# Opening's step 0 loaded as x with slab 0's weights, then the other three slabs', each by SyncE and ScalarE in halves of the rows; slab 0's products first

## The chip, the cores and the metric

The kernel runs on one NeuronCore of a Trainium2 chip. The metric is the device time of one execution in microseconds. All data are float32.

## The reference, cut to what matters

One inference step of a decoder with two layers, for 256 prompt tokens (T) and 8 sample tokens (B), so N = 264 columns of x, each of 1024 features. Layer 0 is a gated short convolution, layer 1 block-sparse attention with a paged cache. The change touches only the start of layer 0 and one store of keys:

```
b_gate, c_gate, h, z = split(x @ w_in, 4, axis=-1)      # w_in: 1024 x 4096
u = c_gate * h
conv = sum(w_conv[j] * up[:, j:j + T] for j in range(3)) # up: earlier rows, then u
y = (b_gate * conv * silu(z)) @ w_out
x = layernorm(alpha * x + y)
...                                                      # layer 1; its new keys k are an output
```

## The kernel before

**Products.** Features lie on the 128 partitions, tokens along the free dimension. Every weight matrix is cut into slabs of 128 output features, 80 in all, numbered n = 0 to 79; a slab holds 8 blocks of 128 x 128, one for each 128 input features (k = 0 to 7). A float32 product is made of three: each operand is split into a high part (a cast to a shorter form, `hi` for weights, `m0h` in the profile for x) and a low part (what is left, `lo` and `m0l`), and high x high, high weight x low x and low weight x high x are added up in PSUM. The casts to the high part are mostly ScalarE's (`act.copy`), the low parts are subtractions on VectorE (`dve.tensor_sub`).

**The opening.** Slabs 0 to 3 and x come together. The tensor `first` has 8 steps k; step k holds 128 rows of 264 columns of x (feature block k) and 4 x 128 columns of the weights of slabs 0 to 3 for that block. Step k needs 12 products: 4 slabs by 3 parts, added to four accumulators. Step 0 and step 1 are each loaded in two pieces by columns, one issued by SyncE (L191, L194) and one by ScalarE (L192, L194); steps 2 to 7 are one DMA each on SyncE's queue (L196). Then come the constants (L197), the page table (L198) and the loads of slabs 4 to 7 (`load`, L112). `first_split(k)` writes the casts of a step in order: x high (L218), weight highs (L222, `high`), x low (L210, `x_low`), weight lows (L225, `low`). The loop over k at L471 then writes TensorE's products: high weights by x high and x low at L475, low weights by x high at L478. Each engine runs its own instructions in the order written.

**Ahead of it** `keep_warm(WARM)` gives TensorE eight products of 512 bf16 columns on constants (L80), with no use of their result.

**After it** `begin(n)` and `mm` go slab by slab (n = 4 to 79) over a table of slots: `at(n, phase, f)` puts a step f into slot n, and `begin(n)` runs the phases of that slot in a fixed order ("dma" first). TensorE's products of slab n are at L139 to L141, the casts of a later slab at L127 (high, ScalarE) and L132 (low, VectorE). With S = 40, `k_store(h, n)` stores the rotated keys of n heads from head h on, on SyncE's queue (L640); heads 2 and 3 go together at slot S + 18, the others singly, head 6 at S + 21 and head 7 at S + 22.

Of the kernel before, what the change touches and what calls it, by code (L numbers as in the profile page):

```python
# [21 lines left out]
N = T + B  # L22
# [2 lines left out]
NPAGE = 20  # L25
ALPHA = math.sqrt(2.0)
EPS = 1e-5
WARM = 8
NKV = 10
EARLY = (40, 41, 42)  # L30
LATE = (78, 79)
# [18 lines left out]
def build(tc, a):  # L50
    nc = tc.nc
    pe, act, dve, pool, sp = nc.tensor, nc.scalar, nc.vector, nc.gpsimd, nc.sync

    with ExitStack() as top:
# [10 lines left out]
        def acc_tile():  # L65
            return acc_full()[:, 0:N + 2]
# [10 lines left out]
        def keep_warm(n):  # L77
            wt = big_tile("warmp")
            for _ in range(n):
                pe.matmul(wt[:, 0:512], one[:, 0:128], one, start=True, stop=True)  # L80

        keep_warm(WARM)

# [20 lines left out]
        raws, his, los = {}, {}, {}  # L104
# [41 lines left out]
        def at(n, phase, f, *args):  # L146
            hooks.setdefault((n, phase), []).append(lambda: f(*args))
# [31 lines left out]
        def begin(n, end=True):  # L179
            for ph in ("dma", "pe", "s0", "hi", "lo", "s1a", "s1b", "s1", "s1c"):  # L180
                run(n, ph)
            if end:
                split_late(n)
# [4 lines left out]


        fst = [ex.tile([128, N + 512], F32, name=f"first{k}") for k in range(8)]  # L190
        sp.dma_start(fst[0][:, 0:N + 128], a["first"][0, :, 0:N + 128])  # L191
        act.dma_start(fst[0][:, N + 128:], a["first"][0, :, N + 128:])  # L192
        for eng, c in ((sp, np.s_[:, 0:N + 256]), (act, np.s_[:, N + 256:])):
            eng.dma_start(fst[1][c], a["first"][1][c])  # L194
        for k in range(2, 8):
            sp.dma_start(fst[k], a["first"][k])  # L196
        sp.dma_start(cst[:, 0:C_ID], a["cst"][:, 0:C_ID])  # L197
        sp.dma_start(pt, a["pt"])  # L198
# [10 lines left out]
        def x_low(k):  # L209
            dve.tensor_sub(pair[0][1][:, k, 0:N], fst[k][:, 0:N], pair[0][0].bitcast(F32)[:, k, 0:N])  # L210

        def first_split(k):
            if k % 2 == 0:
                for d, c in ((his, "hi"), (los, "lo")):
                    d[k // 2] = wp.tile([128, 8, 128], F32R, tag=c, bufs=6, name=f"{c}{k // 2}")
            h, l = his[k // 2], los[k // 2]
            r = 4 * (k % 2)
            act.copy(pair[0][0][:, k, 0:N], fst[k][:, 0:N])  # L218
            raw = fst[k][:, N:].rearrange("p (s m) -> p s m", m=128)

            def high(eng, s0, s1):
                eng(h[:, r + s0:r + s1], raw[:, s0:s1])  # L222

            def low(s0, s1):
                dve.tensor_sub(l[:, r + s0:r + s1], raw[:, s0:s1], h.bitcast(F32)[:, r + s0:r + s1])  # L225

            if k == 0:
                high(dve.tensor_copy, 0, 1)
                high(dve.tensor_copy, 1, 2)
                high(act.copy, 2, 4)  # L230
            elif k == 1:
                high(act.copy, 0, 2)
                high(act.copy, 2, 4)
            elif k == 2:
                high(dve.tensor_copy, 0, 2)
                high(act.copy, 2, 4)
            else:
                high(act.copy, 0, 4)
            x_low(k)
            for s0, s1 in ((0, 2), (2, 4)) if k < 2 else ((0, 4),):  # L240
                low(s0, s1)

        for k in range(8):
            first_split(k)
# [224 lines left out]
        accs = [acc_tile()[:, 0:N], acc_tile()[:, 0:N], two[:, 0:N], two[:, 512:512 + N]]  # L469
        cs_prep()  # L470
        for k in range(8):  # L471
            mh, ml = pair[0][0][:, k, 0:N], pair[0][1][:, k, 0:N]
            for s, c in [(s, c) for c in range(2) for s in range(4)] if k in (0, 2) else [(s, c) for s in range(4) for c in range(2)]:
                wh = his[k // 2][:, (k % 2) * 4 + s, :]
                pe.matmul(accs[s], wh, (mh, ml)[c], start=k == 0 and c == 0, stop=False)  # L475
            for s in range(4):
                wl = los[k // 2][:, (k % 2) * 4 + s, :]
                pe.matmul(accs[s], wl, mh, start=False, stop=k == 7)  # L478
        begin(3)
        ORDER = (2, 1, 3, 0)  # L480
        for s in range(4):
# [56 lines left out]
        with tc.tile_pool(name="l1", bufs=1) as p1, ExitStack() as late_pool:  # L538
# [324 lines left out]
            S = 40  # L863
# [6 lines left out]
                at(S + (11, 11, 12, 12, 15, 15, 16, 16)[h], "s1", rows_back, 0, h)  # L870
                at(S + (13, 13, 14, 14, 18, 19, 20, 21)[h], "s1", rows_back, 1, h)
            for h in range(8):
                if h not in (2, 3):
                    at(S + (15 if h < 4 else 19) + h % 4, "dma", k_store, h)
                at(S + 18 + h, "dma", v_store, h)

            at(S + 18, "dma", k_store, 2, 2)
            at(S + 3, "s1", zero_fill)
            for h0, n, ph in ((0, 6, "s0"), (4, 8, "s1")):
                at(S + n, ph, s_rope, qs, h0, h0 + 4)  # L880
# [194 lines left out]
            for i in range(2, 32):  # L1075
# [13 lines left out]
                h = i % 8  # L1089
# [51 lines left out]
            for k in range(8):  # L1141
                for c in range(2):
                    for j in range(4):
                        pe.matmul(ps[32 * j:32 * j + 32], gs[:, c, k, :],  # L1144
                                  wide(raws, k)[:, 256 * j + 128 * c:256 * j + 128 * c + 128],
                                  start=k == 0 and c == 0, stop=False)
# [93 lines left out]
```

## Time and profile before

| | us |
|---|---|
| median of 3 runs | 275.22 (275.09 to 276.06) |
| the profiled execution's own time | 275.37 |
| its span | 273.6 |
| TensorE busy in the span | 268.7 |
| VectorE, ScalarE, GpSimd busy | 203.0, 170.9, 65.9 |
| mean DMA rate over the span | 243 GB/s |

Times in profile rows count from the start of the span. A row of the timeline has start, duration, engine, line of the code, operation, output <- inputs and count, and in brackets how long the engine had been idle and what ended that. SPq is SyncE's queue of DMA issues; a row of it is the issue, not the transfer. PE is TensorE, PEld its weight loads, ACT ScalarE, DVE VectorE, POOL GpSimd. Matmuls are pipelined: a row's duration is longer than the pitch between two of them.

### The profile page before, as it was taken

Reading aid. Unit: us, or ns where it says so; the run is one execution under the profiler, and the core shown is the slowest. Engines: PE = TensorE matmul, PEld = TensorE weight load, DVE = VectorE, ACT = ScalarE, POOL = GpSimd, SP = SyncE. Lnnn points to the kernel's source line nnn. Section 1 sums busy time; section 2 is a strip of 40 time slices with the busy share of each in tenths; the row PEclk is TensorE's granted clock in tenths of the full one; section 3 lists DMA queues with packets and bytes.
Section 4 is the critical chain, followed back from the end, with each engine's and each line's share of the span. In section 5 each row is a group of like instructions: output and inputs, shape, how many; then the busy total and the mean of one; then the engine's idle time right before and its main releaser. Section 6 shows DMA issues by size and latency. Waiting matters only on the chain.

```text
span 273.6 us, 6278 instructions
## 1 busy us (share of the span) xinstructions
PE 268.7 (98%) x2307; PEld 251.9 (92%) x2307; DVE 203.0 (74%) x414; ACT 170.9 (62%) x349; POOL 65.9 (24%) x129
## 2 busy tenths in 40 slices
PE   8999999999999999999999999999999999999994
PEld 5999999999999999999997997999959987998883
DVE  3978966655875857979999858699847583994745
ACT  4886554453655628549587765988846954599302
POOL 1121432020110101961323365621100020000122
PEclk9999999999999999999999999999999999999999
DMA  7976789999775875132223999997989955781012
GB/s 246 409 274 225 268 291 320 399 396 379 244 257 196 278 234 188 57 149 77 80 77 101 364 404 386 357 338 235 351 320 305 407 195 172 237 276 61 1 77 89
DMA packets 24336, 66.48 MB, mean 243 GB/s; under 512 B 3058, under 2 KB 6898, under 8 KB 24178
## 3 DMA queue, kind: packets, MB, share of 16 engines
q1 hardware_dynamic: 23874, 65.69, 67.6%
q10 hardware_dynamic: 432, 0.39, 0.5%
q8 instruction: 18, 0.29, 0.4%
q14 instruction: 12, 0.10, 0.1%
HBM read 61.67 MB, written 3.35 MB: 238 GB/s over the span
## 4 chain that ended last, share of the span: by engine, by line
PE 96%; DMA 2%; ACT 0%; SPq 0%; DVE 0%; issue 0%
PE acc L139 24%; PE acc L141 24%; PE acc L140 24%; PE c L1023 4%; PE sd L758 3%; PE dps L809 3%; PE acc L475 2%; PE acc L1023 2%; PE c1b L1023 2%; DMA first<-first 2%; PE so L1144 1%; PE acc L478 1%; PE s L692 1%; PE o L730 1%; PE pt L720 1%; PE s L690 1%
## 5 line engine op out<-in xcount | busy, mean ns | idle before, releaser
L127 ACT CAST hi<-raw 128x1024 fp32r<-128x1024 f32 x76 | 79.2, 1050 | 34.0 <-DMA raw<-w 18.9
L132 DVE TENSOR_TENSOR lo<-raw,hi 128x1024 fp32r<-128x1024 f32 x76 | 92.7, 1227 | 6.7 <-ACT hi L127 6.2
L139 PE MATMUL acc<-m0h,hi 128*128 128x264 f32 (+1 forms) x280 | 79.4, 283 | 0.0
L141 PE MATMUL acc<-m0l,hi 128*128 128x264 f32 (+1 forms) x280 | 79.3, 283 | 0.0
L140 PE MATMUL acc<-m0h,lo 128*128 128x264 f32 (+1 forms) x280 | 78.9, 282 | 0.0
L139 PE MATMUL acc<-m1h,hi 128*128 128x264 f32 x264 | 76.4, 289 | 0.0
L141 PE MATMUL acc<-m1l,hi 128*128 128x264 f32 x264 | 74.6, 282 | 0.0
L140 PE MATMUL acc<-m1h,lo 128*128 128x264 f32 x264 | 74.5, 282 | 0.0
L140 PEld LDWEIGHTS acc<-m0h,lo 128*128 128x128 f32 x280 | 52.7, 188 | 0.0
L139 PEld LDWEIGHTS acc<-m0h,hi 128*128 128x128 f32 x280 | 52.6, 188 | 0.1
L141 PEld LDWEIGHTS acc<-m0l,hi 128*128 128x128 f32 x280 | 52.5, 188 | 0.0
L139 PEld LDWEIGHTS acc<-m1h,hi 128*128 128x128 f32 x264 | 49.6, 188 | 1.7 <-issue 0.8
L140 PEld LDWEIGHTS acc<-m1h,lo 128*128 128x128 f32 x264 | 49.8, 189 | 0.0
L141 PEld LDWEIGHTS acc<-m1l,hi 128*128 128x128 f32 x264 | 49.6, 188 | 0.0
L431 POOL COPY uo<-up 128x10 f32<-128x10 f32 x8 | 8.0, 1003 | 64.2 <-DVE up L430 58.4
L648 POOL COPY vs<-vh 128x8 f32<-128x8 f32 x8 | 3.3, 408 | 32.5 <-ACT vh L647 32.5
L701 DVE CUSTOM_DVE_ANT_0 P<-s,cst 128x128 f32<-128x128 f32 (+1 forms) x16 | 5.1, 354 | 5.8 <-PE s L692 5.8
L439 DVE SCALAR_TENSOR_TENSOR t<-up,cst,t 128x256 f32<-128x256 f32 x8 | 3.9, 482 | 7.1 <-ACT t L438 7.1
L838 POOL COPY zs<-z 128x8 f32<-128x8 f32 x8 | 3.0, 377 | 24.4 <-ACT z L837 24.4
L837 ACT ACTIVATE z<-acc 128x264 f32<-128x264 f32 x8 | 3.1, 385 | 9.1 <-PE acc L141 9.1
L965 ACT ACTIVATE zq<-raw 128x1024 f32<-128x1024 f32 x8 | 8.5, 1058 | 0.1
L591 POOL COPY qs<-q 128x8 f32<-128x8 f32 x7 | 4.0, 577 | 17.7 <-ACT q L590 13.0
(230 smaller groups left out, 443.6 us busy)
## 6 DMA issues: line engine op xcount, KB each, us to landing
raw<-w SPq DMA_DIRECT2D x76, 512.0 KB, 4.6
kv<-kc SPq DMA_DIRECT2D x32, 256.0 KB, 6.0
kv<-vc SPq DMA_DIRECT2D x16, 512.0 KB, 6.7
first<-first SPq DMA_DIRECT2D x6, 388.0 KB, 6.7
v_o<-vh SPq DMA_DIRECT2D x8, 132.0 KB, 5.5
xf<-kall SPq DMA_DIRECT2D x16, 64.0 KB, 2.6
kall<-gb SPq DMA_DIRECT2D x1, 1024.0 KB, 6.0
k_o<-kall SPq DMA_DIRECT2D x6, 132.0 KB, 4.5
```

The lines of the kernel that those rows point to most:

```text
L127: act.copy(his[n][sl], raws[n][sl])
L132: dve.tensor_sub(los[n][sl], raws[n][sl], his[n].bitcast(F32)[sl])
L139: pe.matmul(acc, wh, mh[:, k, 0:w], start=first and k == ks[0], stop=False)
L140: pe.matmul(acc, wl, mh[:, k, 0:w], start=False, stop=False)
L141: pe.matmul(acc, wh, ml[:, k, 0:w], start=False, stop=last and k == ks[-1])
L431: pool.tensor_copy(uo[:, f], up[:, T:N + 2])
L475: pe.matmul(accs[s], wh, (mh, ml)[c], start=k == 0 and c == 0, stop=False)
L701: dve.tensor_tensor_reduce(out=P[sl], in0=s_ps[h][sl], in1=mask[sl], scale=-SCALE, scalar=3e38, op0=ALU.add, op1=ALU.min, accum_out=mx[:, ...
L758: pe.matmul(s[32 * j:32 * j + 16, 0:256], zq[:, o:o + 16], kt, start=step == 0 and i == 0, stop=step == 3 and i == 3)
L809: pe.matmul(dps[0][32 * j:32 * j + 32, 512 * c:512 * c + 512], pm[b2][pg][:, j, :], kv_tiles[step, j][:, 512 * c:512 * c + 512], start=ste ...
L965: act.activation(od, wide(raws, k), AF.Copy, accum_out=wsum[:, k:k + 1])
L1023: pe.matmul(acc, g[m][:, k, t], wide(d, k)[:, c0:c1], start=k == 0 and i == 0, stop=k == 7 and i == 2)
```

## The change

Step 0 is now loaded in four pieces: x with slab 0's weights (columns 0 to 391), then slabs 1 to 3 (columns 392 to 775), each in two halves of 64 rows, the upper by SyncE and the lower by ScalarE. Step 1 becomes one DMA on SyncE's queue, like steps 2 to 7. The casts of step 0 get an order of their own: VectorE casts slab 0 high, then takes x low and slab 0's low; ScalarE casts slab 1 and slabs 2 and 3 high; VectorE takes the lows of slab 1 and of slabs 2 and 3. TensorE's step 0 does slab 0's three products first, then the other slabs', part by part. For the other steps the order of the products is as before, written in another way. `keep_warm` gives six products instead of eight. The keys of heads 6 and 7 are stored by one DMA at slot S + 22.

```diff
-WARM = 8
+WARM = 6
...
-        sp.dma_start(fst[0][:, 0:N + 128], a["first"][0, :, 0:N + 128])
-        act.dma_start(fst[0][:, N + 128:], a["first"][0, :, N + 128:])
-        for eng, c in ((sp, np.s_[:, 0:N + 256]), (act, np.s_[:, N + 256:])):
-            eng.dma_start(fst[1][c], a["first"][1][c])
-        for k in range(2, 8):
+        for c in (slice(0, N + 128), slice(N + 128, N + 512)):
+            for eng, p in ((sp, slice(0, 64)), (act, slice(64, 128))):
+                eng.dma_start(fst[0][p, c], a["first"][0, p, c])
+        for k in range(1, 8):
             sp.dma_start(fst[k], a["first"][k])
...
             if k == 0:
                 high(dve.tensor_copy, 0, 1)
-                high(dve.tensor_copy, 1, 2)
+                x_low(k)
+                low(0, 1)
+                high(act.copy, 1, 2)
                 high(act.copy, 2, 4)
-            elif k == 1:
+                low(1, 2)
+                low(2, 4)
+                return
+            if k == 1:
...
-            for s, c in [(s, c) for c in range(2) for s in range(4)] if k in (0, 2) else [(s, c) for s in range(4) for c in range(2)]:
-                wh = his[k // 2][:, (k % 2) * 4 + s, :]
-                pe.matmul(accs[s], wh, (mh, ml)[c], start=k == 0 and c == 0, stop=False)
-            for s in range(4):
-                wl = los[k // 2][:, (k % 2) * 4 + s, :]
-                pe.matmul(accs[s], wl, mh, start=False, stop=k == 7)
+            if k == 0:
+                steps = [(0, c) for c in range(3)] + [(s, c) for c in range(3) for s in range(1, 4)]
+            elif k == 2:
+                steps = [(s, c) for c in range(3) for s in range(4)]
+            else:
+                steps = [(s, c) for s in range(4) for c in range(2)] + [(s, 2) for s in range(4)]
+            for s, c in steps:
+                w = (los if c == 2 else his)[k // 2][:, (k % 2) * 4 + s, :]
+                pe.matmul(accs[s], w, ml if c == 1 else mh, start=k == 0 and c == 0, stop=k == 7 and c == 2)
...
-                if h not in (2, 3):
+                if h not in (2, 3, 6, 7):
...
+            at(S + 22, "dma", k_store, 6, 2)
```

## The prediction

> **What bounds the kernel now.** I read the page first, then the waits of TensorE, then the chain of waits, and only then the first 17 us of the timeline, because the change lies there.
>
> ```profile
> span 273.6 us, 6278 instructions
> PE 268.7 (98%) x2307; PEld 251.9 (92%) x2307; DVE 203.0 (74%) x414; ACT 170.9 (62%) x349; POOL 65.9 (24%) x129
> ...
> PE 96%; DMA 2%; ACT 0%; SPq 0%; DVE 0%; issue 0%
> ```
>
> TensorE is busy for 98% of the span and holds 96% of the chain. The one other thing on the chain is a DMA, 2%. So time can be won only where TensorE stands still, and the waits say where that is.
>
> ```profile
> PE acc L475 <- ACT m0h L218: 0.2, 1, 0.2
> ...
> PEld acc L475 <- ACT m0h L218: 1.2, 2, 0.9
> ```
>
> The products of the opening (L475) wait for x's casts, and the wait stands twice on the weight loads. The chain says what lies behind it:
>
> ```profile
> 1.69 5.44 DMA first<-first
> 7.12 0.02 issue
> 7.15 0.42 ACT m0h L218
> 7.57 0.04 issue
> 7.61 0.39 PE acc L475
> ```
>
> The DMA that is issued at 1.69 is the first of the six at L196, so step 2 of the opening, not step 0. It lands at 1.69 + 5.44 = 7.13; ScalarE casts x (0.42), and step 2's products start at 7.61. All TensorE work after that follows without a gap until the tail. So what counts is when step 2 starts, and the change works on step 0.
>
> ```profile
> 0.78 3.36 PE L80 MATMUL warmp<-const-bfloat16-1.0 128*128 128x512 bf16 x8 [0.78 <-PEq L1221]
> ...
> 2.95 0.20 ACT L205 ACTIVATE dummy<-epst 128x1 f32<-128x1 f32 x1
> ...
> 3.84 0.41 ACT L218 CAST m0h<-first 128x264 fp32r<-128x264 f32 x1 [0.69 <-DMA first<-first]
> 3.84 0.36 DVE L222 CAST hi<-first 128x128 fp32r<-128x128 f32 x2 [3.84 <-DMA first<-first]
> ...
> 4.30 0.81 PE L475 MATMUL acc<-m0h,hi 128*128 128x264 f32 x4 [0.17 <-ACT m0h L218]
> ...
> 4.72 0.41 ACT L218 CAST m0h<-first 128x264 fp32r<-128x264 f32 x1 [0.16 <-DMA first<-first]
> ...
> 5.04 0.71 ACT L222 CAST hi<-first 128x256 fp32r<-128x256 f32 x2
> ...
> 5.44 0.64 PE L478 MATMUL acc<-m0h,lo 128*128 128x264 f32 x4
> ...
> 5.92 0.28 PE L475 MATMUL acc<-m0h,hi 128*128 128x264 f32 x1
> ...
> 6.87 0.64 PE L478 MATMUL acc<-m0h,lo 128*128 128x264 f32 x4
> ...
> 8.15 0.42 ACT L218 CAST m0h<-first 128x264 fp32r<-128x264 f32 x1 [0.28 <-DMA first<-first]
> ...
> 8.47 0.61 ACT L222 CAST hi<-first 128x512 fp32r<-128x512 f32 x1
> ...
> 9.27 0.28 PE L475 MATMUL acc<-m0h,hi 128*128 128x264 f32 x1
> ```
>
> Four products in 0.64 with one of 0.28 as their end give a pitch of 0.12. Step 0 runs from 4.30 to 5.92, step 1 from 5.92 to 6.87 + 4 x 0.12 = 7.35. From 7.35 to 7.61 TensorE waits for step 2. Step 3's weight cast ends at 8.47 + 0.61 = 9.08 and its first product is at 9.27, so step 3 would let TensorE be at most about 0.14 earlier (with 0.05 from a cast's end to the product, as 7.57 to 7.61).
>
> How much had passed when step 2 landed is in the table by stretch (the last column is GB/s):
>
> ```profile
> 1.50:2.50 1.00, 1.00 (x4) 0.36 (x3) 0.00 (x0) 0.85 (x1) 0.23 (x3) 1.00 0.66 205
> 1.50:3.00 1.50, 1.50 (x5) 0.59 (x4) 0.00 (x0) 1.34 (x2) 0.23 (x3) 1.00 0.79 256
> 1.50:4.00 2.50, 2.50 (x7) 0.76 (x5) 0.16 (x2) 1.65 (x3) 0.23 (x3) 1.00 0.94 314
> 4.00:6.50 2.50, 2.33 (x18) 2.19 (x18) 2.32 (x8) 1.58 (x5) 0.00 (x0) 1.00 0.92 310
> 6.50:9.00 2.50, 2.40 (x19) 2.18 (x18) 1.70 (x4) 1.57 (x4) 0.00 (x0) 1.00 1.01 394
> ```
>
> One step is 128 x 776 x 4 bytes = 397 kB. Steps 0 to 2 are 1192 kB. 785 kB had passed at 4.0 (2.5 x 314), and the other 407 kB need 1.31 at 310 GB/s: their bytes are through at about 5.3, yet step 2 lands at 7.13. So it lands late because its last parts come behind bytes of later steps, and because the stream is slow there (310 against 394). Nothing in the change touches either directly.
>
> **The change, part by part.**
>
> Step 0's transfers. x and slab 0's weights are 392 columns, 201 kB, where now all 397 kB compete from the start. 205 kB are through at 2.50, 384 at 3.00, so the whole step's bytes at about 3.05. If landing follows bytes, x and slab 0 land 0.55 earlier than the 3.84 at which the casts start now: 3.29. It can't help before 3.15, where ScalarE ends its table and dummy (2.95 + 0.20), and at the worst the halves land no earlier, 3.84. I take 3.3, by the bytes. Issues: ScalarE two before and two after. SyncE has nine for this tensor instead of eight.
>
> Step 0's casts and products. Cost of a 128-column piece comes from the two shapes that the trace has:
>
> ```profile
> L225 DVE TENSOR_TENSOR lo<-first,hi 128x512 fp32r<-128x512 f32 x6 | 4.2, 706 | 0.1
> L210 DVE TENSOR_TENSOR m0l<-first,m0h 128x264 fp32r<-128x264 f32 x8 | 3.5, 442 | 0.2
> ...
> L222 ACT CAST hi<-first 128x256 fp32r<-128x256 f32 x4 | 1.5, 400 | 0.0
> L225 DVE TENSOR_TENSOR lo<-first,hi 128x256 fp32r<-128x256 f32 x4 | 1.5, 419 | 0.0
> ```
>
> VectorE: 0.42 at 256 and 0.71 at 512, so about 0.28 for 128. ScalarE: 0.40 at 256 and 0.61 at 512, so about 0.30. ScalarE casts x from 3.30 to 3.71, then waits for the second piece (by 3.84 at the latest, when the whole step is there now), casts slab 1 to 4.14 and slabs 2 and 3 to 4.54. It is free before step 1's x (4.72), so its added 0.30 is hidden; without that gap of 0.18 it would delay step 1's casts. VectorE: x low after 3.71 to 4.18 (0.44), slab 0's low to 4.46, slab 1's to 4.74, slabs 2 and 3 to 5.16, free when step 1's x cast ends (4.72 + 0.41 = 5.13). Products: slab 0 by x high at 3.76, by x low at 4.2, its low at 4.5. In the written order everything else of step 0 stands behind that third product, so nine more at 0.12 follow: step 0 ends at 4.5 + 10 x 0.12 = 5.70, 0.22 earlier than 5.92. Step 1's weights are cast by 5.04 + 0.36 = 5.40, so step 1 goes from 5.70 to 7.14. If the halves land at 3.84 the same sum gives 6.24 and 7.68; at 3.15, 5.55 and 6.99.
>
> Step 2. Its bytes and their order are the same, on the same queue. With step 2 landing at 7.13 its products start at 7.61 and the 0.21 of step 1 turn into a longer wait (0.26 grows to 0.47). Ends: landing at 3.84 loses 7.68 - 7.61 = 0.07, landing at 3.15 gains nothing. Value: 0. If step 2 alone came a little sooner, step 3's casts allow 0.14. Step 1's whole rows of 3104 bytes in place of two pieces can bring it forward a little; I take 0.1 of the 0.14.
>
> The queue of SyncE:
>
> ```profile
> 1.20 0.44 SPq L194 DMA_DIRECT2D first<-first  x1
> 1.69 3.70 SPq L196 DMA_DIRECT2D first<-first  x6
> ...
> 6.17 0.36 SPq L198 DMA_DIRECT2D pt<-pt  x1
> 7.14 20.86 SPq L112 DMA_DIRECT2D raw<-w  x11
> ```
>
> Step 2 is issued after three instead of two, one pitch (from step 1's issue at 1.20 to the next at 1.69, 0.49) later, as are the constants and page table behind it. The page table's issue ends at 6.53, and the weight load behind it starts only at 7.14, when step 2 lands: 0.6 of slack hides 0.49, and without it the weight loads would slip by the rest. Step 2's own issue is the open part: between 0 (the stream's bytes decide) and 0.49 later. I take 0, as the six issues fit in 3.70 while steps land about 1.0 apart (7.13 and, by the casts, 8.15): a landing follows bytes, not its issue.
>
> The two warm products less. Six end at about 0.78 + 6 x 0.42 = 3.30, so they free TensorE before 3.76. Their cost depends on the clock. Eight products of 512 columns in 3.36 are 0.42 each, 1.2 columns per ns. The opening's 264 columns in 0.12 are 2.2. So full speed comes between these, though the clock column reads 1.00 throughout. If it comes as soon as now, the cost is 0. If it comes later, see the rivals.
>
> The store of keys. Heads 6 and 7 go as one, at the slot of head 7:
>
> ```profile
> L640 SPq DMA_DIRECT2D k_o<-kall x7: 369/385/425, 171.3 to 204.2; - x7
> ```
>
> SyncE saves one issue of 0.385 us; head 6's bytes leave one slot later, 69 us before the end. TensorE's list of waits has no wait there, so 0 either way; TensorE's products of that stage hide it.
>
> **Sum.** The profiled execution took 275.37, its span 273.6. Transfers 0, products 0 (bounds +0.07 and -0.14), issues 0 (bound +0.49), warm products 0, store 0, step 2 a little sooner -0.1: 275.27 against 275.37. The median of the runs is 275.22, 0.15 lower, so I forecast 275.1.
>
> **Rivals.** *Step 2 no longer lags (gain).* If the transfers spread more evenly, step 2 could land at 5.3 + 0.8 = 6.1 (0.8 is what step 0 takes from its bytes' passing, 3.05, to the casts, 3.84), and step 3 as much sooner. Then step 1's end decides: 7.14 for 7.61, a gain of 0.47; at the best landing 6.99, 0.62. It stops at the first weight slab (a group of the page, then the timeline):
>
> ```profile
> L132 DVE TENSOR_TENSOR lo<-raw,hi 128x1024 fp32r<-128x1024 f32 x76 | 92.7, 1227 | 6.7 <-ACT hi L127 6.2
> ```
> ```profile
> 14.69 3.85 DVE L132 TENSOR_TENSOR lo<-raw,hi 128x1024 fp32r<-128x1024 f32 x3 [0.81 <-ACT hi L127]
> ...
> 16.48 0.28 PE L139 MATMUL acc<-m0h,hi 128*128 128x264 f32 x1
> ```
>
> Its low part ends at 14.69 + 1.23 = 15.9, so TensorE can reach it 0.6 to 0.7 earlier at most. Time 274.7. For it: the lag of 1.0 is no property of step 2's own bytes. Against: the edit does not change what is queued from step 2 on.
>
> *The clock (slower).* Six products and then gaps (one at 3.76, one at 4.2, one at 4.5) may not bring full speed as soon as eight without a gap. If full speed came at 7.5 (between 3.3 and 5.0 now, and one warm stretch of 3.36 later), step 0 would run at 0.22 a product, 264 columns at 1.2: 4.5 + 10 x 0.22 = 6.7, and 3.6 products of step 1 by 7.5, the other 8.4 at 0.12 by 8.5: +0.9, so 276.1. At 6.7 it is +0.5, at 8.3 +1.3. It decides from about 5.5, where the 21 products left at 4.72 just end at 7.61. For: the six fill only 2.5 of the 3.36 that the eight fill. Against: the wait from 7.35 to 7.61 left the pitch at 0.12, and products go on from 3.76.
> The Trainium skill speaks for this rival: its page "TensorE: Matmul & The Clock Gate", in "Part 1: The HAM clock gate", has the array at half speed until a free-running window of about 3.4 us has been busy. This trace agrees with the half speed and with the 3.36 of warm products before the fast ones. By that page of the Trainium skill six products alone do not fill the window, and with one window more the sum would be about +0.9 (an estimate) instead of 0. No run here shows yet how busy a window must be.
>
> *Step 2 lands later.* Its issue decides after all: +0.45, 275.65. For: it goes fourth, not third, on SyncE. Against: the landings 1.0 apart.
>
> *The halves gain nothing.* Then TensorE starts at 4.30 and the sum is +0.07, inside the likeliest case.
>
> **How the numbers follow.** Likeliest, the landing of step 2 decides as now: 0.52, 275.1 (its own range 274.9 to 275.4). Step 2 without its lag: 0.23, 274.7. Clock late: 0.17, 276.0. Step 2 later: 0.08, 275.65. The range 274.5 to 276.0 holds all but the later half of the clock's cases and the noise beyond the best landing. About 0.5%, 1.38 us, is what a measurement of this kernel can tell from no change. The greatest gain, 0.65, is far below it, so faster has 0.04 for what I have not seen; slower needs the clock later than 8.4, about a third of its 0.17 and a little for the unseen: 0.07; same 0.89.
>
> **What would show it.** Right: first product near 3.8, step 0's end near 5.7, the wait before step 2 longer, step 2 again near 7.6, first L139 product near 16.4. Wrong: step 2's x cast well before 7.15 (second case); 264-column products 0.22 apart after 4.5 (clock); step 2's cast at 7.6 (issue). A time outside 274.5 to 276.0 would mean that something beyond the opening moved.

## The result and the profile after

The change made the kernel slower: 277.29 us (median of 6 runs, 276.88 to 277.61) against 275.48 (6 runs, 275.09 to 276.06). The ratio is 1.0066, 95% interval 1.0055 to 1.0078, so about 1.8 us. The time lies above the range that was predicted (274.5 to 276.0), on the other side of the forecast.

The page after has the same shape as before; TensorE's share did not fall, it is busy 1.5 us longer with two products fewer:

```profile
span 275.4 us, 6279 instructions
PE 270.2 (98%) x2305; PEld 253.6 (92%) x2305; DVE 202.8 (74%) x414; ACT 171.1 (62%) x350; POOL 63.8 (23%) x129
...
PE 97%; DMA 1%; ACT 0%; DVE 0%; issue 0%; ACTq 0%
```

TensorE is busy longer with fewer products, so single products got longer. The chain of waits up to the first slab shows where:

```profile
0.74 2.76 DMA first<-first
...
3.58 0.42 ACT m0h L217
...
4.05 14.40 PE acc L485 x96
```

Before, step 2's transfer ended the wait at 7.15. Now the chain goes back to step 0's own first piece, and from 4.05 on TensorE's 96 products of the opening are one piece: behind it nothing on the chain waits for a transfer. But they take 14.40. At the pitch of 0.12 they would take 11.5. The timeline of the changed kernel shows both halves of the story (the products of the opening are now all at L485, x's cast at L217, the weight cast at L221):

```profile
0.74 1.21 ACTq L193 DMA_DIRECT2D first<-first  x2
0.74 1.48 SPq L193 DMA_DIRECT2D first<-first  x2
...
0.78 2.72 PE L80 MATMUL warmp<-const-bfloat16-1.0 128*128 128x512 bf16 x6 [0.78 <-PEq L1229]
...
1.98 1.28 ACT L204 ACT_TABLE_LOAD   x1 [1.98 <-issue]
...
3.58 0.41 ACT L217 CAST m0h<-first 128x264 fp32r<-128x264 f32 x1
...
4.05 0.59 PE L485 MATMUL acc<-m0h,hi 128*128 128x264 f32 x1 [0.55 <-ACT m0h L217]
...
4.52 0.59 PE L485 MATMUL acc<-m0l,hi 128*128 128x264 f32 x1
...
4.84 0.60 ACT L221 CAST hi<-first 128x128 fp32r<-128x128 f32 x2 [0.84 <-DMA first<-first]
4.90 0.42 PE L485 MATMUL acc<-m0h,lo 128*128 128x264 f32 x1
...
5.19 1.11 PE L485 MATMUL acc<-m0h,hi 128*128 128x264 f32 x3
...
6.36 0.41 ACT L217 CAST m0h<-first 128x264 fp32r<-128x264 f32 x1 [0.92 <-DMA first<-first]
...
8.74 0.42 PE L485 MATMUL acc<-m0h,hi 128*128 128x264 f32 x1
8.96 0.35 PE L485 MATMUL acc<-m0l,hi 128*128 128x264 f32 x1
...
9.15 0.64 PE L485 MATMUL acc<-m0h,lo 128*128 128x264 f32 x4
...
18.29 0.28 PE L139 MATMUL acc<-m0h,hi 128*128 128x264 f32 x1
```

Two things are to be seen. First, from 8.74 to 8.96 two neighbours are 0.22 apart, half speed; from 9.15 four take 0.64, a pitch of 0.12. Full speed came about 5 us after the first product, while before it was there from the first one. Second, the transfers are later, not earlier: step 0's second piece is cast at 4.84 (before, the last high weights of step 0 were cast by 4.16 + 0.40 = 4.56), step 1's x at 6.36 instead of 4.72. The first product of slab 4 is at 18.29 against 16.48: 1.81 of the 1.91 between the two profiled executions (277.28 and 275.37) is lost in the opening.

The table by stretch, with stretches that the prediction used, shows the slow start of the stream in its last column (164 GB/s from 1.5 to 4.0, where it was 314):

```profile
1.50:4.00 2.50, 2.00 (x5) 0.45 (x3) 0.23 (x1) 1.90 (x3) 0.23 (x3) 1.00 0.70 164
4.00:6.50 2.50, 2.45 (x8) 2.08 (x9) 1.35 (x4) 0.74 (x3) 0.00 (x0) 1.00 0.95 310
6.50:9.00 2.50, 2.50 (x14) 2.50 (x13) 2.20 (x6) 1.66 (x6) 0.00 (x0) 1.00 0.98 330
```

The column ahead of the last two is the granted clock. It reads 1.00 in all three, also where the products are 0.22 apart: in the first microseconds the pitch has to be read, not this column.

The answers by line give what one issue costs: the half-row issues of the changed kernel first, then two rows and two lines of the kernel before.

```profile
L193 ACTq DMA_DIRECT2D first<-first x2: 568/589/610, 0.7 to 1.3; - x2
L193 SPq DMA_DIRECT2D first<-first x2: 591/710/830, 0.7 to 1.4; - x2
```
```profile
0.74 0.40 ACTq L192 DMA_DIRECT2D first<-first  x1
0.75 0.40 SPq L191 DMA_DIRECT2D first<-first  x1
```
```profile
L937 SPq DMA_DIRECT2D xf<-kall x16: 587/595/1108, 227.7 to 240.0; - x16
L112 SPq DMA_DIRECT2D raw<-w x76: 327/328/810, 7.1 to 240.6; - x76
```

570 to 830 ns for a half of the rows, where whole rows took 400 to 450. The kernel before held a hint: its moves of 32 rows (L937) cost 595 ns to issue, its loads of 128 rows 328. It is no more than a hint, because the moves at L937 go from tile to tile and differ from loads in more than their rows. The prediction did not read that line.

### The profile page after: what moved, and what is told of

It is laid out like the page before. It is cut to its first block, busy times and chain, and to the rows that moved or that the text cites. A ratio compares the mean times of both kernels' runs of the same rounds, so it can differ in the third digit from the quotient of the medians.

```text
span 275.4 us, 6279 instructions
## 1 busy us (share of the span) xinstructions
PE 270.2 (98%) x2305; PEld 253.6 (92%) x2305; DVE 202.8 (74%) x414; ACT 171.1 (62%) x350; POOL 63.8 (23%) x129
## 4 chain that ended last, share of the span: by engine, by line
PE 97%; DMA 1%; ACT 0%; DVE 0%; issue 0%; ACTq 0%
PE acc L139 24%; PE acc L141 24%; PE acc L140 24%; PE acc L485 5%; PE c L1031 4%; PE sd L765 3%; PE dps L816 3%; PE acc L1031 2%; PE c1b L1031 2%; PE so L1152 1%; PE s L699 1%; PE o L737 1%; DMA first<-first 1%; PE pt L727 1%; PE s L697 1%; PE o L738 1%
## 5 line engine op out<-in xcount | busy, mean ns | idle before, releaser
L655 POOL COPY vs<-vh 128x8 f32<-128x8 f32 x8 | 2.4, 305 | 33.1 <-ACT vh L654 33.1
L485 PE MATMUL acc<-m0h,hi 128*128 128x264 f32 x32 | 9.1, 330 | 0.5 <-ACT m0h L217 0.5
L485 PE MATMUL acc<-m0l,hi 128*128 128x264 f32 x32 | 8.8, 322 | 0.0
```

What stands on the lines that cost most here:

```text
L485: pe.matmul(accs[s], w, ml if c == 1 else mh, start=k == 0 and c == 0, stop=k == 7 and c == 2)
```

## The experiments

Two losses were suspected: the clock (six warm products and a gap) and the transfers (halves of the rows). The first four runs cross them. Each ratio is against runs of the kernel before on the same chip. A profile shows one execution of each, so what the other executions did is known by their times alone.

**Eight warm products in the changed kernel.**

```diff
-WARM = 6
+WARM = 8
```

> The changed kernel with eight warm products again. Clock theory (six warm products leave the array at half speed until a later window is busy; that is the whole loss): full speed from about 4.2 us, products of 264 columns 0.12 apart from the first on, median about 275.3. Transfer theory (the half-row loads bring slabs 1 to 3 and step 1 late; the clock costs nothing): the same 277.3 as the changed kernel. Both together: step 1's casts still at about 6.4 to 7.4, so step 1 ends at about 8.5 and the rest follows, 0.7 over the kernel before: 276.2.

276.45 (275.9 to 276.7, 9 runs), ratio 1.0028 (1.0016 to 1.0039): between the kernel before and the changed one, near what both theories together gave. Its timeline:

```profile
4.03 0.59 PE L485 MATMUL acc<-m0h,hi 128*128 128x264 f32 x1
...
5.23 0.60 ACT L221 CAST hi<-first 128x128 fp32r<-128x128 f32 x2 [1.26 <-DMA first<-first]
...
5.58 0.81 PE L485 MATMUL acc<-m0h,hi 128*128 128x264 f32 x3 [0.35 <-ACT hi L221]
...
6.09 0.41 ACT L217 CAST m0h<-first 128x264 fp32r<-128x264 f32 x1 [0.25 <-DMA first<-first]
...
6.59 0.52 PE L485 MATMUL acc<-m0h,lo 128*128 128x264 f32 x3
...
17.12 0.28 PE L139 MATMUL acc<-m0h,hi 128*128 128x264 f32 x1
```

Three products in 0.52 are full speed. Full speed was not there from the first product on, as the clock theory had expected: the products at 4.03 and 4.49 took 0.59 each, as in the changed kernel. That cost nothing here, since TensorE stood for 0.35 behind slab 0 until slab 1's weights were cast. The second piece is cast later still than in the changed kernel (5.23 against 4.84), step 1's x a little earlier (6.09 against 6.36). Slab 4 starts at 17.12: 1.17 of the 1.81 are back, 0.64 are not.

**Six warm products in the kernel before.**

```diff
-WARM = 8
+WARM = 6
```

> The kernel before with six warm products, nothing else. Clock theory: an idle 1.0 us from 3.3 to 4.3, then products 0.22 apart for one stretch of about 3.4 us or more; 1.3 to 2.0 over before, 276.8 to 277.5. Transfer theory: no change, 275.5.

276.99 in the median, ratio 1.0043 (1.0019 to 1.0067), but the ten runs lie between 275.12 and 278.15, more than twice the spread of the kernel before (274.9 to 276.24 in 19 runs). The profiled execution was one that lost nothing (275.12):

```profile
4.17 0.81 PE L475 MATMUL acc<-m0h,hi 128*128 128x264 f32 x4 [0.67 <-DVE hi L222]
4.82 0.64 PE L475 MATMUL acc<-m0l,hi 128*128 128x264 f32 x4
```

Full speed at once, after the same six products and a gap of 0.67, which is longer than the changed kernel's 0.55. So six warm products do not always lose: three of the ten runs are at 275.12 to 275.54, the other seven at 276.54 to 278.15. The expectation had a narrow range of loss (276.8 to 277.5); the wide spread is what it missed.

**The loads of before in the changed kernel** (new order, six warm products).

```diff
-        for c in (slice(0, N + 128), slice(N + 128, N + 512)):
-            for eng, p in ((sp, slice(0, 64)), (act, slice(64, 128))):
-                eng.dma_start(fst[0][p, c], a["first"][0, p, c])
-        for k in range(1, 8):
+        sp.dma_start(fst[0][:, 0:N + 128], a["first"][0, :, 0:N + 128])
+        act.dma_start(fst[0][:, N + 128:], a["first"][0, :, N + 128:])
+        for eng, c in ((sp, np.s_[:, 0:N + 256]), (act, np.s_[:, N + 256:])):
+            eng.dma_start(fst[1][c], a["first"][1][c])
+        for k in range(2, 8):
```

> The changed kernel with the loads of before, so the new order, six warm products and the joined store. Clock theory: first product near 4.3 after 1.0 us of idle, 0.22 apart until a later window; 276.8 to 277.5. Transfer theory: 275.3 to 275.5.

277.06 (276.81 to 277.49, 4 runs), ratio 1.0051 (1.0034 to 1.0068). The loads are the old ones and most of the loss is still there. The timeline has the late clock by itself:

```profile
4.23 0.59 PE L486 MATMUL acc<-m0h,hi 128*128 128x264 f32 x1 [0.73 <-ACT m0h L218]
...
7.72 0.42 PE L486 MATMUL acc<-m0h,hi 128*128 128x264 f32 x1
...
7.94 0.42 PE L486 MATMUL acc<-m0l,hi 128*128 128x264 f32 x1
...
8.34 0.28 PE L486 MATMUL acc<-m0l,hi 128*128 128x264 f32 x1
...
8.46 0.28 PE L486 MATMUL acc<-m0h,hi 128*128 128x264 f32 x1
```

0.22 apart at 7.72, 0.12 apart at 8.34.

**The new order alone** (the loads of before, as in the run above, and eight warm products in the changed kernel; the joined store of keys is in it too).

```diff
-WARM = 6
+WARM = 8
```

> The new order of casts and products and the joined store, with the loads of before and eight warm products. By the theory of two losses (late full speed and slow half-row loads) neither is here: 275.5 to 275.8, same as before. If the order itself costs (slab 0's third product stands ahead of nine others, and three waits thin out TensorE's work before full speed), step 0 ends 0.2 to 0.3 later and some runs get full speed late: 276.0 to 276.5.

275.52 (275.25 to 276.07, 10 runs), ratio 1.0003 (0.9989 to 1.0016). The order and the store cost nothing that shows. Beside the run above it, this one differs in two warm products alone: 277.06 against 275.52, with like runs of the kernel before (275.74 and 275.51). The same two products cost about 1.3 to 1.5.

In the new order the four combinations are now complete. Two warm products fewer raise the ratio from 1.0003 to 1.0051 with the loads of before and from 1.0028 to 1.0066 with the changed loads; the changed loads raise it from 1.0003 to 1.0028 with eight warm products and from 1.0051 to 1.0066 with six.

**Four warm products in the kernel before.**

```diff
-WARM = 8
+WARM = 4
```

> The kernel before with four warm products. Clock theory (full speed comes at the end of a window of about 3.4 us that was busy enough, and where the windows lie differs from run to run): no window that holds the gap from 2.5 to 4.2 can be busy enough, so every run is late by most of a window: 277.0 to 278.5 in all, and the products 0.22 apart until 7 to 10 us. If the number of warm products does nothing: 275.7.

277.25 (276.19 to 277.71, 4 runs), ratio 1.0066 (1.0043 to 1.009). The profiled execution, the best of the four, was at half speed for its first 13 products, of which these are the first four (0.81 in the kernel before):

```profile
4.19 1.25 PE L475 MATMUL acc<-m0h,hi 128*128 128x264 f32 x4 [1.54 <-DVE hi L222]
```

The spread reaches lower than expected.

**Ten warm products in the kernel before.**

```diff
-WARM = 8
+WARM = 10
```

> The kernel before with ten warm products. Clock theory: no gap ahead of the first product, full speed in the same window as with eight or sooner, the last warm products short once it has come; first product 0.0 to 0.7 later, mostly inside the wait for step 2: 275.4 to 275.9, with no run above 276.5. If the number of warm products only delays: 0.86 later, 276.3.

275.53 (275.15 to 276.05, 10 runs), ratio 0.9999 (0.999 to 1.0008). Two more cost nothing that shows. The expectation gave a reason, a delay hidden in the wait for step 2, and the trace does not bear it out:

```profile
4.06 0.41 ACT L218 CAST m0h<-first 128x264 fp32r<-128x264 f32 x1 [0.90 <-DMA first<-first]
...
4.52 0.91 PE L475 MATMUL acc<-m0h,hi 128*128 128x264 f32 x4
...
7.19 0.64 PE L478 MATMUL acc<-m0h,lo 128*128 128x264 f32 x4
...
7.67 0.65 PE L475 MATMUL acc<-m0h,hi 128*128 128x264 f32 x4
```

The first product is at 4.52 instead of 4.30 when x's cast, which also started 0.22 later here, has just ended (4.06 + 0.41). There was no wait for step 2: 7.19 and four products at 0.12 give 7.67. So four, six, eight and ten give 277.25, 276.99, 275.5 to 275.7 and 275.53: once eight keep TensorE busy up to the first product, more gain nothing.

**The changed loads alone in the kernel before** (its old order, eight warm products).

```diff
-        sp.dma_start(fst[0][:, 0:N + 128], a["first"][0, :, 0:N + 128])
-        act.dma_start(fst[0][:, N + 128:], a["first"][0, :, N + 128:])
-        for eng, c in ((sp, np.s_[:, 0:N + 256]), (act, np.s_[:, N + 256:])):
-            eng.dma_start(fst[1][c], a["first"][1][c])
-        for k in range(2, 8):
+        for c in (slice(0, N + 128), slice(N + 128, N + 512)):
+            for eng, p in ((sp, slice(0, 64)), (act, slice(64, 128))):
+                eng.dma_start(fst[0][p, c], a["first"][0, p, c])
+        for k in range(1, 8):
```

> The kernel before with the changed loads alone (halves of the rows, step 1 as one DMA), eight warm products, the old order. Transfer theory: issues of about 0.6 to 0.8 us instead of 0.4, step 0's second piece at about 4.8, step 1 at about 6.3; the opening ends 0.7 to 1.0 later, 276.2 to 276.5. Clock theory alone: 275.5, or a little less.

276.66 (276.26 to 277.82, 5 runs), ratio 1.0045 (1.0021 to 1.0069). After one product at 4.24 TensorE stood for 1.38 until slab 1's weights were cast:

```profile
6.00 0.67 PE L474 MATMUL acc<-m0h,hi 128*128 128x264 f32 x3 [1.38 <-DVE hi L221]
```

The issues took 0.57 to 0.83. Two of the five runs, at 277.51 and 277.82, lie 0.9 and 1.2 above the highest of the other three (276.66); no trace shows why.

**Is it the halves of the rows?** Step 0 in two DMAs of 64 rows with all columns; all else is the kernel before.

```diff
-        sp.dma_start(fst[0][:, 0:N + 128], a["first"][0, :, 0:N + 128])
-        act.dma_start(fst[0][:, N + 128:], a["first"][0, :, N + 128:])
+        for eng, p in ((sp, slice(0, 64)), (act, slice(64, 128))):
+            eng.dma_start(fst[0][p], a["first"][0, p])
```

> The kernel before with step 0 in two DMAs of 64 rows and all 776 columns, one by SyncE and one by ScalarE; nothing else changed. If the half-row form is slow: each issue 0.57 or more against 0.40, the whole step in later than 3.84, at 4.5 or so, rate from 1.5 to 4.0 well under 314 GB/s; 276.0 to 276.4. If only the number of pieces is: issues near 0.40, landing by 3.8, 275.6.

276.29 (275.93 to 277.56, 10 runs), ratio 1.0038 (1.0019 to 1.0057). Its timeline and its table by stretch:

```profile
0.74 0.59 SPq L192 DMA_DIRECT2D first<-first  x1
0.74 0.56 ACTq L192 DMA_DIRECT2D first<-first  x1
...
1.35 0.59 ACTq L194 DMA_DIRECT2D first<-first  x1
1.39 0.81 SPq L194 DMA_DIRECT2D first<-first  x1
...
5.18 0.41 ACT L218 CAST m0h<-first 128x264 fp32r<-128x264 f32 x1 [1.71 <-DMA first<-first]
```
```profile
1.50:4.00 2.50, 2.50 (x7) 0.73 (x5) 0.00 (x0) 1.49 (x2) 0.23 (x3) 1.00 0.79 206
```

Two DMAs as before, the same bytes, only cut by rows and not by columns: 0.56 to 0.59 an issue for 0.40, and the whole-row issues behind them (L194) also take longer, 0.59 and 0.81 for 0.44 and 0.45. Step 0 is cast at 5.18 for 3.84, and the stream moves 206 GB/s for 314. The halves are slow by themselves: this execution had full speed from its first products on. It is one of seven at 275.93 to 276.40. The other three are at 277.48 to 277.56; a late full speed would fit them, but no trace of such a run shows it, and the ratio of 1.0038 holds both kinds.

**Whole rows, both pieces of step 0 by SyncE** (new order, eight warm products, step 1 in one DMA).

```diff
-            for eng, p in ((sp, slice(0, 64)), (act, slice(64, 128))):
-                eng.dma_start(fst[0][p, c], a["first"][0, p, c])
+            sp.dma_start(fst[0][:, c], a["first"][0, :, c])
```

> The new order with eight warm products, and step 0 in the same two column pieces but in whole rows of 128, both by SyncE; step 1 one DMA. If it is the halves of the rows that make the loads slow: issues of 0.40 to 0.45 again, x and slab 0 landed by 3.3, the second piece by 4.0, step 1 by 5.0, and 275.3 to 275.7. If it is the four pieces or step 1 as one DMA that is slow: the second piece near 4.8 and step 1 near 6.3 as in the changed kernel, 276.3 to 276.6.

276.51 (276.24 to 277.08, 10 runs), ratio 1.0036 (1.0025 to 1.0047). The expectation was wrong in half:

```profile
3.33 0.41 ACT L216 CAST m0h<-first 128x264 fp32r<-128x264 f32 x1 [1.09 <-DMA first<-first]
...
6.20 0.41 ACT L216 CAST m0h<-first 128x264 fp32r<-128x264 f32 x1 [1.84 <-DMA first<-first]
...
6.97 0.39 PE L484 MATMUL acc<-m0h,hi 128*128 128x264 f32 x1 [1.04 <-ACT hi L220]
```

x with slab 0 is there at 3.33, half a microsecond earlier than before, as the change meant it, and with short issues (two in 0.88). But step 1 came at 6.20 and TensorE stood for 1.04. An early step 0 was worth nothing here, because step 1 did not follow.

**Step 1 as one DMA, nothing else.**

```diff
-        for eng, c in ((sp, np.s_[:, 0:N + 256]), (act, np.s_[:, N + 256:])):
-            eng.dma_start(fst[1][c], a["first"][1][c])
-        for k in range(2, 8):
+        for k in range(1, 8):
```

> The kernel before with one change: step 1 as one DMA on SyncE's queue, step 0 in its two column pieces of whole rows. If step 1 as one DMA is late by itself (it landed for a cast at 6.2 with whole rows on SyncE alone): x of step 1 cast at about 6, TensorE waits about 0.7 to 1.0 before step 1, 276.2 to 276.6. If the lateness came from SyncE carrying all the bytes alone or from the half rows: step 1 cast by 5.0, 275.5.

275.58 (275.02 to 275.92, 10 runs), ratio 1.0001 (0.9992 to 1.001). Step 1's x was cast at 4.80, not at 6:

```profile
4.80 0.41 ACT L216 CAST m0h<-first 128x264 fp32r<-128x264 f32 x1
```

So step 1 as one DMA is not late by itself. In the run before it step 1 was also issued about 0.5 later, third on SyncE's queue instead of second, and cast 1.4 later; why it lagged that much with SyncE as the only issuer stays open.

**Step 2 in two pieces like step 1.**

```diff
-        for eng, c in ((sp, np.s_[:, 0:N + 256]), (act, np.s_[:, N + 256:])):
-            eng.dma_start(fst[1][c], a["first"][1][c])
-        for k in range(2, 8):
+        for k in (1, 2):
+            for eng, c in ((sp, np.s_[:, 0:N + 256]), (act, np.s_[:, N + 256:])):
+                eng.dma_start(fst[k][c], a["first"][k][c])
+        for k in range(3, 8):
```

> The kernel before with step 2 also in two column pieces, one by SyncE and one by ScalarE, like step 1. If a step lands early because two queues feed it: step 2 cast well before 7.15, no wait of TensorE between steps 1 and 2, a gain of at most 0.26 of that wait plus what step 3's casts allow, 275.1 to 275.4 beside 275.5. If step 3, as the first step in one DMA, now lags in its place: the wait moves to step 3 and the time is the same, 275.5 to 275.8.

275.67 (275.42 to 276.12, 12 runs), ratio 1.0006 (0.9997 to 1.0015). Step 2's x was cast at 7.20 (7.15 in the kernel before):

```profile
7.20 0.41 ACT L219 CAST m0h<-first 128x264 fp32r<-128x264 f32 x1 [0.93 <-DMA first<-first]
```

Feeding step 2 from two queues did not bring it earlier in this execution, and the time is the same. No version that I ran beats the kernel before.

## Why the prediction was wrong, point by point

**Warm products, taken at 0: the first step that failed.** The sum let full speed come as soon with six products as with eight. The clock rival had the mechanism, with a chance of 0.17 and +0.9, and it was the larger of the two losses. By the profiles it cost 1.17 in the opening (18.29 against 17.12); by times 1.3 to 1.5 with the old loads. The rival's own arithmetic held: it gave +1.3 for full speed at 8.3, and with the old loads full speed came at about 8.3 and the time was 1.32 longer (277.06 against 275.74). My argument against it, that the wait from 7.35 to 7.61 had left the pitch at 0.12, was no evidence: a gap of 0.26 at full speed says nothing on a gap of 0.55 before it is reached. "Products go on from 3.76" was also weak: at 4.05, 4.52 and 4.90 TensorE had little to do. The condition that I named, full speed later than 5.5, was met (about 9.1), and the pitch of 0.22 after 4.5 that I named as its sign is in the timeline.

The Trainium skill's rule that I weighed there ("TensorE: Matmul & The Clock Gate", "Part 1: The HAM clock gate") agrees with the half speed behind six warm products, and its free-running window would explain ten runs of one kernel between 275.12 and 278.15; no run here shows the window itself. The runs add that six products and a gap of 0.67 can be enough (275.12) or not, and that four gave 276.19 at best. All six runs of the changed kernel and all four with its order and the old loads were slow, while three of ten runs with the old order and six warm products were not; whether the new order makes the loss surer or this was chance is not shown.

**Step 0's transfers, the whole step there by 3.84 at the latest and step 1 as before: the second step that failed.** I counted bytes and kept the price of an issue. The first piece kept the bound (x was cast at 3.58), the rest did not. The halves took 0.57 to 0.83 an issue instead of 0.40 to 0.45, the stream ran at 164 GB/s instead of 314, the second piece was cast at 4.84, and step 1's x at 6.36 where the sum kept 4.72. The bound was no bound, because I took the price of a whole-row issue for a new form; a sign of a higher one stood in the trace at L937. ScalarE's longer issues also moved its table load from 1.65 to 1.98, so x could not have been cast before 3.47 (the dummy behind it starts at 3.27 and takes 0.20). In the runs the loads alone cost a ratio of 1.0045, the halves alone 1.0038, and 1.0028 was left in the changed kernel with eight warm products. The first two of these hold runs near 277.5 whose further loss is not explained. The losses overlap: at half speed TensorE reached step 1 only at 7.42, when the late step 1 was already cast, so they do not add up.
The Trainium skill, "DMA: Bandwidth & Descriptors", "Rules for kernel authors", advises against two transfers to disjoint halves of the partitions, because both run on the same 16 engines. The runs agree: with step 0 in two such halves the median was 276.29 against 275.51.

**Step 2 decides: true for one profiled execution of the kernel before, not for the changed kernel.** With slower products TensorE was never ahead of step 2, and the wait that I expected to grow is gone from the chain. The reading was also too firm for the kernel before: step 2's landing is no fixed time. In six traces with the loads of before its x was cast at 6.06 to 7.15, and the prediction rested on the latest of them. In the traces of the new order alone, of ten warm products and of step 1 as one DMA no product of step 1 or 2 waited for a transfer; the opening ran on from its first product at 4.35 to 4.52, so there its start decided.

**What held.** The added casts and the joined store cost nothing that shows (the new order alone at 1.0003). That an earlier step 0 buys nothing is not shown: the one run with x early (3.33, whole rows by SyncE) had a late step 1, and an early step 0 with steps 1 and 2 on time was not run. The bound for a gain, at most 0.65, was not touched by any run. The added issue ahead of the weight loads did move them (7.59 for 7.14), with no wait of TensorE for it in the list.

**The chances.** 0.07 for slower by over 0.5% was far too low. I let the two open prices, the clock and the form of the load, stand at their hoped-for ends, and both fell on the other side.

## What to carry to other kernels

Where TensorE is warmed up ahead of the first transfer, the warm products should last until the first real product: here two too few made the time at which full speed comes differ from execution to execution, and two more than needed cost nothing that shows. Price a DMA by a row of the same form, rows and all, wherever the trace has one; bytes alone do not give it. And before a first step is made earlier, look which later step ends the wait: an earlier start only helps if everything up to that step is earlier too. Look in more than one execution, since a transfer that ended the wait in one profile did not in others.

## What the runs showed of the hardware that was not expected

- A load of 64 rows is slower to issue than one of 128: 0.56 to 0.59 us against 0.40, and the whole-row issues behind it grew from 0.45 and 0.44 to 0.59 and 0.81. Why is not settled here.
- With SyncE issuing alone, in whole rows, step 1 landed for a cast at 6.20; with ScalarE issuing one piece of step 0 beside it, at 4.80, though step 1 was one DMA on SyncE's queue in both (third there in the first run, second in the other).
- With the same loads, landings differ between executions: step 2's x was cast at 6.06 to 7.15 in six traces, step 1's at 4.72 to 5.32.
- The granted clock reads 1.00 in stretches where products run at half speed; only the pitch (0.22 against 0.12 for 264 columns) shows it.
